# A ragged layer norm: who issues the first loads and the lengths, and TensorE's program unrolled in place of a loop

## The chip, the core and the metric

The kernel runs on one core of one Trainium2 chip. The metric is device time in microseconds (us). Before the change the median of three runs is 258.67 us (258.59 to 258.95).

## What is computed

`x` is a batch of 32 sequences of 512 rows with 1024 floats each; `lengths` says how many rows of each sequence are real (64 to 511).

```python
def reference(x, lengths, gamma, beta, eps):
    output = np.zeros_like(x)
    for b in range(batch):
        x_b = x[b, :lengths[b]]
        mean = np.mean(x_b, axis=-1, keepdims=True)
        var = np.var(x_b, axis=-1, keepdims=True)
        output[b, :lengths[b]] = (x_b - mean) / np.sqrt(var + eps) * gamma + beta
    return output
```

Rows past a sequence's length are zero, and need not be read.

## The kernel before

**Tiles.** A unit is 4 rows (16 KB). The first 64 rows of every sequence are always real; they make 4 static tiles of 128 units, one unit in each of the 128 partitions (2 MB a tile). All further units that hold a real row are numbered one after the other over the batch, from the lengths, and make the dynamic tiles; the units that hold none are filled from a tile of zeros `zt`, 128 units to a store. With the lengths of this run there are 19 tiles to normalize and 14 zero stores.

**Half tiles.** A tile is worked on as two half tiles (2 of its 4 rows in each partition; step `t`, 38 of them run). For each: VectorE (DVE) takes the row statistics (`dve_stats`, L396 and L401), ScalarE (ACT) takes the root (L423), DVE makes the reciprocal and the negated mean (L386, L387), ACT normalizes into fp16 `h` (L407), DVE multiplies by gamma (L380), TensorE (PE) adds beta by multiplying `h` with the identity and a row of ones with beta into PSUM (four matmuls each), and ACT writes PSUM back over `x` in SBUF, times the row mask (L416). Three `h` buffers, two PSUM buffers and eight `x` buffers rotate.

**What the lengths start.** DVE's first instruction that needs the lengths is the cast at L233, behind a few small ones that don't. Behind it stand, in DVE's program order, the sums over the lengths and the index tables (L234 to L269, the last one `idx_i`), the cast of the identity (L367), and only then the statistics of half tile 0, of half tile 1, the index of the first store and the masks (L334 to L329), and so on. GpSimd (POOL) waits for `idx_i` before it issues the loads of the dynamic tiles.

**Who issues what.** SyncE (SP) issues the two halves of tile 0 one after the other (L576): each is 1 MB, 8 KB in each partition, and has its own semaphore. ACT issues the lengths (L564: all 32 of them, as 256 bytes, into each of the 128 partitions), then gamma and beta (L565, L566: one partition, 4 KB each), and then starts its own program. POOL issues everything else as indirect DMAs: the loads of tiles 1 to 3 (static indices; L601), of tiles 4 to 7 once `idx_i` is there, then per tile a store (L623 for the two halves of tile 0, L630 for the others), at most one zero store (L637), and the load of the tile that reuses a freed buffer. Tile 1's store waits for the last write-back of half tile 3.

**TensorE's program.** For the 4 static tiles (6 half tiles) the instructions are written out (L442, L448), and wait for fixed counts of the semaphores. From there `run_tensor` runs a loop over three tiles (six half tiles, the period of the three `h` and two PSUM buffers): each half tile waits for counts kept in two registers, issues its eight matmuls (`emit_mm`, L433), adds 9 to the one and 5 to the other register, and after each tile branches on the number of tiles. The other engines have all tiles written out, with a conditional branch after each (`run_engine`).

Of the kernel before, what the change touches and what calls it, by code (L numbers as in the profile page):

```python
# [11 lines left out]
P = 128  # L12
UR = 4
ST_ROWS = 64
R = 8
RH = 3
RM = 4
DVE_STEP = 9
ACT_STEP = 5
ZSTEPS = (0, 1, 2, 3, 4, 5, 7, 9, 11, 13) + tuple(range(15, 32))  # L20

class Program:
# [46 lines left out]
def kernel(tc, x, lengths, gamma, beta, eps, out):  # L69
    nc = tc.nc  # L70
    B, T, D = x.shape
# [3 lines left out]
    NST = B * S0 // P  # L75
# [4 lines left out]
    NH = 2 * (NT + 1)  # L80
    CH = 512
    assert (B, T, D) == (32, 512, 1024)

    sem = {e: tc.alloc_semaphore(f"s_{e}") for e in ("DVE", "ACT", "PE", "POOL")}
    s_len = tc.alloc_semaphore("s_len")
    s_row = tc.alloc_semaphore("s_row")
    s_xs = [tc.alloc_semaphore(f"s_xs{i}") for i in range(2)]
# [13 lines left out]
    with pool_cm as sb, psum_cm as psb:  # L101
        def st(shape, dt, name):
            return sb.tile(shape, dt, name=name)

        xt = [st([P, UR * D], FP32, f"x{i}") for i in range(R)]
        ht = [st([P, 2, D], FP16, f"h{i}") for i in range(RH)]
        zt = st([P, UR * D], mybir.dt.bfloat16, "zt")
        len64 = st([P, B], mybir.dt.int64, "len64")
        row_f = st([1, 2 * D], FP32, "row_f")
        row_h = st([1, 2 * D], FP16, "row_h")  # L110
        gamma_h = st([P, D], FP16, "gamma_h")
        ones_h = st([1, P], FP16, "ones_h")
        idn_f = st([P, P], FP32, "idn_f")
        idn_h = st([P, P], FP16, "idn_h")
# [56 lines left out]
        ps = [psb.tile([P, 2, D], FP32, name=f"ps{i}") for i in range(2)]  # L171
# [4 lines left out]
        dve, act, pe, pool, sp = nc.vector, nc.scalar, nc.tensor, nc.gpsimd, nc.sync  # L176
        pr = Program(sem)
        add = pr.add

        def iota(t, pattern, base=0, mult=0):  # L180
# [9 lines left out]
            out=sidx[:, :], in0=p4_i[:, 0:1].broadcast_to([P, NST]), scalar=float(U - S0), in1=sb_i[:, :],  # L190
# [9 lines left out]
            out=idn_f[:, :], in_=idn_f[:, :], compare_op=OP.not_equal, fill=1.0,  # L200
            base=0, pattern=[[-1, P]], channel_multiplier=1), [a_i0])
        for t in range(2, R):
# [7 lines left out]
               for i, f in enumerate(fields)]  # L210
        d_k2 = add("DVE", lambda: dve.tensor_tensor(out=k_i[:, 0:2], in0=k_i[:, 0:2], in1=k_i[:, 2:4],
                                                    op=OP.bitwise_or), [d_k[3]])
        d_k1 = add("DVE", lambda: dve.tensor_tensor(out=k_i[:, 0:1], in0=k_i[:, 0:1], in1=k_i[:, 1:2],
                                                    op=OP.bitwise_or), [d_k2])
        d_dk = add("DVE", lambda: dve.tensor_tensor(out=dk_f[:, :], in0=k_i[:, 0:1], in1=p_i[:, :],
                                                    op=OP.subtract), [d_k1])
# [148 lines left out]
        tok = {}  # L365
# [58 lines left out]
                out=sq[r][:, :], in_=mv[r][:, :, 1], func=AF.Sqrt, bias=eps_sb[:, 0:1], scale=1.0),  # L424
                [tok["stats", t]])

        def emit_mm(t):
            h, p_ = ht[t % RH], ps[t % 2]
            for w, lhs in ((idn_h, None), (ones_h, row_h)):
                for j in range(2):  # L430
                    for c in range(2):
                        rhs = h[:, j, c * CH : c * CH + CH] if lhs is None else row_h[:, D + c * CH : D + c * CH + CH]
                        ins = pe.matmul(p_[:, j, c * CH : c * CH + CH], w[:, :], rhs,  # L433
                                        start=lhs is None, stop=lhs is not None)
            ins.then_inc(sem["PE"], 1)

        def pe_mm(t):
            h, p_ = ht[t % RH], ps[t % 2]
            first = [tok["mul", t], tok.get(("evac", t - 2)), tok["idn"], c_gam]
            for j in range(2):  # L440
                for c in range(2):
                    add("PE", lambda j=j, c=c: pe.matmul(  # L442
                        p_[:, j, c * CH : c * CH + CH], idn_h[:, :], h[:, j, c * CH : c * CH + CH],
                        start=True, stop=False), first, inc=False)
                    first = []
            for j in range(2):
                for c in range(2):
                    tok["pe", t] = add("PE", lambda j=j, c=c: pe.matmul(  # L448
                        p_[:, j, c * CH : c * CH + CH], ones_h[:, :], row_h[:, D + c * CH : D + c * CH + CH],
                        start=False, stop=True), [], inc=(j == 1 and c == 1))  # L450
# [22 lines left out]
        def emit_op(e, name, op):  # L473
            _, fn, waits, inc = op
            for key, val in waits:
                e.wait_ge(handles[key], val)
            ins = fn()
            if inc:
                ins.then_inc(sem[name], 1)

        def units_register(e, name):

            r = e.alloc_register(f"{name}_nd")
            e.wait_ge(sem["DVE"], d_tot[1])
            e.reg_load(r, tot_i[0:1, 0:1])
            return r

        def tiles_register(e, r):

            e.reg_add(r, r, P - 1)  # L490
            e.reg_alu(r, r, 7, OP.arith_shift_right)
            e.reg_add(r, r, NST)

        def run_engine(e, name, block, setup=None):
            base = nc.cur_bb
            guards = []
            r = None
            if setup is not None:
                setup()
            for op in pr.ops[name]:  # L500
                if op[0] == "op":
                    emit_op(e, name, op)
                else:
                    k = op[1]
                    if k == 2 * NST - 1:
                        r = units_register(e, name)
                        tiles_register(e, r)
                    if k >= 2 * NST + 1 and k % 2 == 1 and k < NH - 1:
                        nxt = f"{name}_s{k + 1}"
                        e.br_lt(r, (k + 1) // 2, f"{name}_exit", nxt)  # L510
                        for g in guards:
                            g.__exit__(None, None, None)
                        guards = [nc.bb(nxt, parent=base)]
                        guards[0].__enter__()
            e.br(f"{name}_exit")
            for g in guards:
                g.__exit__(None, None, None)
            with nc.bb(f"{name}_exit", parent=base):
                e.br(block.end_bb)

        def run_tensor(e, block):


            base = nc.cur_bb
            k0 = 2 * NST
            for op in pr.ops["PE"]:
                if op[0] == "op":
                    emit_op(e, "PE", op)
                elif op[1] == k0 - 1:
                    break  # L530
            r = units_register(e, "PE")
            tiles_register(e, r)
            r_dve, r_act, r_t = (e.alloc_register(f"PE_{n}") for n in ("dve", "act", "t"))
            e.reg_mov(r_dve, tok["mul", k0 - 2][1])
            e.reg_mov(r_act, tok["evac", k0 - 4][1])
            e.reg_mov(r_t, NST)
            for k in range(k0, NH):
                assert tok["mul", k - 2][1] == tok["mul", k0 - 2][1] + (k - k0) * DVE_STEP
                assert tok["evac", k - 4][1] == tok["evac", k0 - 4][1] + (k - k0) * ACT_STEP
            e.br("PE_s0")  # L540
            for i in range(3):
                with nc.bb(f"PE_s{i}", parent=base):
                    for k in (k0 + 2 * i, k0 + 2 * i + 1):
                        e.wait_ge(sem["DVE"], r_dve)
                        e.wait_ge(sem["ACT"], r_act)
                        emit_mm(k - 2)
                        e.reg_add(r_dve, r_dve, DVE_STEP)
                        e.reg_add(r_act, r_act, ACT_STEP)
                    e.reg_add(r_t, r_t, 1)
                    e.br_lt(r, r_t, "PE_exit", f"PE_s{(i + 1) % 3}")  # L550
            with nc.bb("PE_exit", parent=base):
                e.br(block.end_bb)

        with tc.tile_critical():
            with nc.Block() as block:

                @block.vector
                def _(e):
                    run_engine(e, "DVE", block)

                @block.scalar
                def _(e):
                    def setup():
                        e.dma_start(out=len64[:, :], in_=lengths[None, :].to_broadcast([P, B])).then_inc(s_len, 16)  # L564
                        e.dma_start(out=row_f[:, 0:D], in_=gamma[None]).then_inc(s_row, 16)  # L565
                        e.dma_start(out=row_f[:, D : 2 * D], in_=beta[None]).then_inc(s_row, 16)  # L566
                    run_engine(e, "ACT", block, setup)

                @block.tensor
                def _(e):  # L570
                    run_tensor(e, block)

                @block.sync
                def _(e):
                    for h in range(2):
                        e.dma_start(out=xt[0][:, 2 * h * D : 2 * h * D + 2 * D],  # L576
                                    in_=x[4 * h : 4 * h + 4, 0:ST_ROWS].rearrange("b (p r) d -> p b (r d)", r=2)
                                    ).then_inc(s_xs[h], 16)
                    e.br(block.end_bb)

                @block.gpsimd
# [139 lines left out]
```

## Time and profile before

| | |
|---|---|
| median of three runs | 258.67 us |
| the profiled execution's own time | 258.67 us |
| its span (first to last event on the core) | 256.5 us |
| busy in the span: PE, DVE, ACT, POOL | 55%, 70%, 71%, 25% |
| bytes moved by DMA | 105.37 MB, mean 411 GB/s |
| share of the span that DMA packets took: POOL's queue, SP's queue, ACT's queue | 95.9%, 2.1%, 0.1% |

A line of the timeline reads: start in us, duration, engine, line of the kernel, operation, out<-in, how many were merged (x2), and in brackets how long the engine had been idle and what ended that. ACTq, SPq and POOLq are the instruction queues of those engines, where DMAs are issued; the DMA queue of SP is numbered 1 in the page, that of ACT 10, that of POOL 0 and that of the instruction loads 14. In the list of DMA issues the last number is the time in us from issue to landing. In the table by stretches the last two columns are the DMA engines' busy share and GB/s. The trace also has every DMA packet with its queue, start, duration and size, and every step of a semaphore; where packets are spoken of, they are read there. Each of the 16 DMA engines serves all queues.

### The profile page before, as it was taken

The page shows a single profiled execution, that of the slowest core. Times are in us where ns is not written, and L with a number is a line of the kernel's source. Part 1 is how long each engine was busy: PE and PEld are TensorE (multiplying, and loading weights), DVE is VectorE, ACT ScalarE, POOL GpSimd, SP SyncE. Part 2 cuts the span into 40 slices and gives each one's busy share as a digit, 9 for nine tenths or more (in the row PEclk, how much of TensorE's full clock was granted, in tenths as well). Part 3 has the DMA queues.
Part 4 walks back from the last instruction along what each step waited for, and adds up shares of the span by engine and source line. Part 5 has one row for each costly group of instructions (what it writes and reads, how often), then busy time and mean ns, then how long its engine had stood idle before and what let it go on. Part 6 is the DMA issues. An engine that isn't in the chain of part 4 may idle for free.

```text
span 256.5 us, 1653 instructions
## 1 busy us (share of the span) xinstructions
PE 141.7 (55%) x306; PEld 32.4 (13%) x306; DVE 178.9 (70%) x421; ACT 182.9 (71%) x198; POOL 63.3 (25%) x68
## 2 busy tenths in 40 slices
PE   0101908274966678668767786687677867820000
PEld 0000202021211111111111111111111111100000
DVE  3989697987688778877887888678878886820000
ACT  2440756758799989998999899989998999850000
POOL 5183021040523322304112603040307130320000
DMA  4999999999999999999999999999999999999980
GB/s 167 435 437 423 432 424 418 438 434 432 423 443 416 443 419 439 422 437 437 422 429 424 437 424 423 429 436 424 439 419 437 422 437 419 445 423 434 427 353 10
DMA packets 8080, 105.37 MB, mean 411 GB/s; under 512 B 1388, under 2 KB 1388, under 8 KB 1390
## 3 DMA queue, kind: packets, MB, share of 16 engines
q0 software_dynamic: 7632, 103.13, 95.9%
q1 hardware_dynamic: 288, 2.10, 2.1%
q14 instruction: 11, 0.09, 0.1%
q10 hardware_dynamic: 148, 0.04, 0.1%
q8 instruction: 1, 0.02, 0.0%
HBM read 41.98 MB, written 69.21 MB: 433 GB/s over the span
## 4 chain that ended last, share of the span: by engine, by line
DVE 35%; PE 28%; ACT 18%; DMA 5%; issue 3%; POOLq 1%; ACTq 1%; SPq 0%; DVEq 0%; POOL 0%
PE ps_149 L433 23%; DVE stats_132 L396 18%; DMA x_61<-in_x_dram 5%; DVE h_69 L380 3%; DVE h_71 L380 3%; DVE h_70 L380 3%; ACT x_63 L416 3%; ACT x_62 L416 2%; ACT x_61 L416 2%; PE ps_149 L442 2%; PE ps_149 L448 2%; ACT x_68 L416 2%; ACT x_66 L416 2%; ACT x_67 L416 2%; ACT x_64 L416 2%
## 5 line engine op out<-in xcount | busy, mean ns | idle before, releaser
L433 PE MATMUL ps_150<-row_h,ones_h 1*128 1x512 f16 x64 | 30.1, 622 | 0.0
L433 PE MATMUL ps_149<-row_h,ones_h 1*128 1x512 f16 x64 | 30.1, 622 | 0.0
L433 PE MATMUL ps_149<-h_69,idn_h 128*128 128x512 f16 x24 | 11.3, 627 | 11.2 <-DVE h_69 L380 11.2
L380 DVE TENSOR_TENSOR h_69<-h_69,gamma_h 128x2048 f16<-128x2048 f16 x13 | 15.5, 1191 | 0.6 <-DVE mv_136 L401 0.6
L637 POOL DMA_INDIRECT out_dram<-zt,zidx x14 | 14.4, 1031 | 5.3 <-issue 4.0
L380 DVE TENSOR_TENSOR h_70<-h_70,gamma_h 128x2048 f16<-128x2048 f16 x13 | 15.5, 1189 | 0.0
L433 PE MATMUL ps_150<-h_70,idn_h 128*128 128x512 f16 x24 | 11.3, 626 | 6.8 <-DVE h_70 L380 6.8
L380 DVE TENSOR_TENSOR h_71<-h_71,gamma_h 128x2048 f16<-128x2048 f16 x12 | 14.3, 1190 | 0.0
L433 PE MATMUL ps_149<-h_71,idn_h 128*128 128x512 f16 x20 | 9.4, 627 | 8.6 <-DVE h_71 L380 8.6
L433 PE MATMUL ps_149<-h_70,idn_h 128*128 128x512 f16 x20 | 9.4, 627 | 7.9 <-DVE h_70 L380 7.9
L433 PE MATMUL ps_150<-h_71,idn_h 128*128 128x512 f16 x20 | 9.4, 628 | 6.3 <-DVE h_71 L380 6.3
L433 PE MATMUL ps_150<-h_69,idn_h 128*128 128x512 f16 x20 | 9.4, 628 | 6.3 <-DVE h_69 L380 6.3
L386 DVE RECIPROCAL rstd_143<-sq_139 128x2 f32<-128x2 f32 x10 | 1.7, 166 | 13.7 <-ACT sq_139 L423 13.7
L386 DVE RECIPROCAL rstd_141<-sq_137 128x2 f32<-128x2 f32 x10 | 1.7, 166 | 12.7 <-ACT sq_137 L423 12.7
L442 PE MATMUL ps_149<-h_69,idn_h 128*128 128x512 f16 x4 | 1.9, 628 | 14.5 <-DVE h_69 L380 14.5
L433 PEld LDWEIGHTS ps_150<-row_h,ones_h 1*128 1x128 f16 x64 | 6.7, 125 | 22.4 <-issue 22.4
L433 PEld LDWEIGHTS ps_149<-row_h,ones_h 1*128 1x128 f16 x64 | 6.7, 125 | 22.4 <-issue 22.4
L396 DVE BATCH_NORM_STATS2 stats_132<-x_61 128x6 f32<-128x512 f32 x12 | 7.4, 679 | 0.6 <-DMA x_61<-in_x_dram 0.6
L396 DVE BATCH_NORM_STATS2 stats_131<-x_62 128x6 f32<-128x512 f32 x12 | 7.4, 680 | 0.0
L396 DVE BATCH_NORM_STATS2 stats_131<-x_61 128x6 f32<-128x512 f32 x12 | 7.4, 680 | 0.0
L396 DVE BATCH_NORM_STATS2 stats_131<-x_63 128x6 f32<-128x512 f32 x12 | 7.4, 680 | 0.0
L396 DVE BATCH_NORM_STATS2 stats_131<-x_64 128x6 f32<-128x512 f32 x12 | 7.4, 680 | 0.0
(207 smaller groups left out, 384.2 us busy)
## 6 DMA issues: line engine op xcount, KB each, us to landing
x_61<-in_x_dram SPq DMA_DIRECT2D x2, 1024.0 KB, 10.6
out_dram<-zt,zidx POOLq DMA_INDIRECT x14, 23.7
len_73<-in_lengths_dram ACTq DMA_DIRECT2D x1, 32.0 KB, 4.4
x_65<-in_x_dram,idx_i POOLq DMA_INDIRECT x2, 20.3
x_66<-in_x_dram,idx_i POOLq DMA_INDIRECT x2, 19.7
x_67<-in_x_dram,idx_i POOLq DMA_INDIRECT x2, 21.7
x_68<-in_x_dram,idx_i POOLq DMA_INDIRECT x2, 23.7
out_dram<-x_61,fidx POOLq DMA_INDIRECT x2, 14.6
```

The source lines that it names most:

```text
L380: tok["mul", t] = add("DVE", lambda: dve.tensor_tensor(out=h[:, :, :], in0=h[:, :, :], in1=gamma_h[:, None, :].broadcast_to([P, 2, D]), op ...
L386: a = add("DVE", lambda: dve.reciprocal(out=rstd[r][:, :], in_=sq[r][:, :]), [tok["sqrt", t]])
L396: tk = add("DVE", lambda j=j, c=c: dve.bn_stats(out=s[:, j, c, :], in_=xx[:, j * D + c * CH : j * D + c * CH + CH]), [load_dep(t)])
L416: tok["evac", t] = add("ACT", lambda j=j, row=row: act.activation(out=xx[:, j * D : j * D + D], in_=p_[:, j, :], func=AF.Copy, bias=0.0, s ...
L433: ins = pe.matmul(p_[:, j, c * CH : c * CH + CH], w[:, :], rhs, start=lhs is None, stop=lhs is not None)
L442: add("PE", lambda j=j, c=c: pe.matmul(p_[:, j, c * CH : c * CH + CH], idn_h[:, :], h[:, j, c * CH : c * CH + CH], start=True, stop=False) ...
L448: tok["pe", t] = add("PE", lambda j=j, c=c: pe.matmul(p_[:, j, c * CH : c * CH + CH], ones_h[:, :], row_h[:, D + c * CH : D + c * CH + CH] ...
L637: e.indirect_dma_start(out=ou, out_offset=bass.IndirectOffsetOnAxis(ap=zidx[:, g : g + 1], axis=0), in_=zt[:, :], in_offset=None, bounds_c ...
```

## The change

TensorE's loop and what it needs go: PE runs through `run_engine` like the others, with all half tiles written out and fixed wait counts. The second half of tile 0 is issued by ACT ahead of gamma and beta; the lengths are issued by SP behind the first half.

```diff
+        def first_half(e, h):
+            e.dma_start(out=xt[0][:, 2 * h * D : 2 * h * D + 2 * D],
+                        in_=x[4 * h : 4 * h + 4, 0:ST_ROWS].rearrange("b (p r) d -> p b (r d)", r=2)
+                        ).then_inc(s_xs[h], 16)
...
-        def emit_mm(t):
...
-        def run_tensor(e, block):
...
                 @block.scalar
                 def _(e):
                     def setup():
-                        e.dma_start(out=len64[:, :], in_=lengths[None, :].to_broadcast([P, B])).then_inc(s_len, 16)
+                        first_half(e, 1)
                         e.dma_start(out=row_f[:, 0:D], in_=gamma[None]).then_inc(s_row, 16)
                         e.dma_start(out=row_f[:, D : 2 * D], in_=beta[None]).then_inc(s_row, 16)
                     run_engine(e, "ACT", block, setup)
 
                 @block.tensor
                 def _(e):
-                    run_tensor(e, block)
+                    run_engine(e, "PE", block)
 
                 @block.sync
                 def _(e):
-                    for h in range(2):
-                        e.dma_start(out=xt[0][:, 2 * h * D : 2 * h * D + 2 * D],
-                                    in_=x[4 * h : 4 * h + 4, 0:ST_ROWS].rearrange("b (p r) d -> p b (r d)", r=2)
-                                    ).then_inc(s_xs[h], 16)
+                    first_half(e, 0)
+                    e.dma_start(out=len64[:, :], in_=lengths[None, :].to_broadcast([P, B])).then_inc(s_len, 16)
                     e.br(block.end_bb)
```

The instructions of DVE and POOL and their order stay as they are, and so do ACT's behind its three issues; PE executes the same matmuls.

More of the change, by code (lines that the diff above doesn't have):

```diff
@@ L17 @@
 RM = 4
-DVE_STEP = 9
-ACT_STEP = 5
 ZSTEPS = (0, 1, 2, 3, 4, 5, 7, 9, 11, 13) + tuple(range(15, 32))
@@ L425, in act_sqrt @@
                 [tok["stats", t]])
-        def emit_mm(t):
[L428 to L435, printed above, removed]
         def pe_mm(t):
@@ L519, in run_engine @@
                 e.br(block.end_bb)
-        def run_tensor(e, block):
[L524 to L552, printed above, removed]
         with tc.tile_critical():
```

## Prediction

> **What bounds the kernel now.** I read the slices first, then the chain of waits, then the start of the timeline, then POOL's issues. The slices say that the DMA engines are busy from end to end, and the page's sums agree (POOL's queue alone 95.9% of the span).
>
> ```profile
> DMA  4999999999999999999999999999999999999980
> ...
> q0 software_dynamic: 7632, 103.13, 95.9%
> ```
>
> The bytes are fixed, so the time is the bytes' time plus whatever the DMA engines stand idle. They idle at the start (first slice 4 tenths) and in the last 4 us. In between, the question is where the stream is close to running dry. POOL issues all of it in time, except for one place. In the timeline of POOL and the list of DMA issues:
>
> ```profile
> 38.78 1.14 POOL L637 DMA_INDIRECT out_dram<-zt,zidx  x1 [1.32 <-DVE zidx L362]
> 50.76 0.99 POOL L630 DMA_INDIRECT out_dram<-x_62,sidx  x1 [10.84 <-ACT sq_138 L423]
> ```
> ```profile
> out_dram<-zt,zidx POOLq DMA_INDIRECT x14, 23.7
> out_dram<-x_62,sidx POOLq DMA_INDIRECT x1, 8.9
> ```
>
> Tile 1's store lands 8.9 us after its issue at 50.76; no other 2 MB transfer lands as soon. By the packets, its first one starts at 52.77, 2.01 us after the issue, just as the zero store ahead of it ends (53.31 on the last engine). 0.99 us of the 2.01 is the issue instruction itself. So between 0 and 1.02 us of backlog stood ahead of this store: were it later by more than that, the DMA engines would idle, and nothing later gives that back. Tile 2's store starts 3.25 us after its issue, tile 3's 6.92, later ones 11 to 29: behind this place there is cover, and the end is set by bytes.
>
> What leads up to 50.76 is compute without a pause. The chain of waits goes back to the load of tile 0:
>
> ```profile
> 1.61 13.97 DMA x_61<-in_x_dram
> 15.60 2.47 DVE stats_132 L396 x4
> ...
> 18.69 2.86 DVE f_f L296
> ```
>
> From 15.60 on it is only DVE, PE and ACT. So the start of the kernel is on the path, through tile 1's store, although DMA is the bound. And the start reads:
>
> ```profile
> 0.91 0.39 ACTq L564 DMA_DIRECT2D len_73<-in_lengths_dram  x1
> 0.95 1.24 SPq L576 DMA_DIRECT2D x_61<-in_x_dram  x2
> ...
> 5.30 0.18 DVE L233 CAST lenf<-len_73 128x32 f32<-128x32 int32 x1 [2.64 <-DMA len_73<-in_lengths_dram]
> ...
> 11.57 2.47 DVE L396 BATCH_NORM_STATS2 stats_131<-x_61 128x6 f32<-128x512 f32 x4
> ...
> 13.12 0.99 POOL L601 DMA_INDIRECT x_65<-in_x_dram,idx_i  x1 [5.30 <-DVE stats_131 L396]
> ...
> 15.60 2.47 DVE L396 BATCH_NORM_STATS2 stats_132<-x_61 128x6 f32<-128x512 f32 x4 [0.60 <-DMA x_61<-in_x_dram]
> ```
>
> DVE waits for the lengths until 5.30 (landed 5.28), works 6.3 us on indices without a gap, and only then starts half tile 0; POOL's loads of dynamic tiles hang on the same tables. Half tile 1 waits a further 0.6 us for its data.
>
> **The change part by part.**
>
> *The lengths, moved from the head of ACT's queue to behind 1 MB in SP's.* This is the term that counts. When do they land? By the packets, each of the 16 DMA engines carries 8 of the 128 length packets, 8 packets of 8 KB of each half of tile 0 (0.309 us each), and a closing 4-byte packet per transfer. In SP's queue the lengths come behind half 0 on every engine, and half 1 now competes from ACT's queue.
> - An engine's packets ran back to back from about 3.4 us (earliest) to 4.95 (latest) before, the late ones being those on which the lengths came late. I take the slowest engine at 3.6 to 4.9. By the time POOL's first packets come (7.23 to 8.04 before), an engine at 3.6 has done about 13 of its 16 packets of the two halves, one at 4.9 about 10.
> - From there queues alternate packet by packet: before, POOL's packets on one engine started every 0.913 us, that is one of 16 KB (0.611) and one of SP's 8 KB. So the last packets of half 0 and its closing one cost one turn of POOL each: half 0 closes at about 9.7 for the one engine, 11.7 for the other.
> - Then the eight lengths and their closing packet. **Two readings.** (a) In one turn: before, on all 16 engines, the first packet of x started 6 ns after the lengths' closing packet and none stood between; they ran as an unbroken nine. One turn of POOL (0.61) and 0.1 to 0.4 us for the nine (0.015 each, or the 0.055 at which the first engine's came), and 0.35 from last packet to semaphore (before: beta's 6.95 to 7.29): 10.8 to 13.1, middle 11.8. (b) Packet by packet: beta's closing packet came 0.30 us after its data had ended, one packet of x between; POOL's would cost nine turns of 0.625, 5.6 us: 15.7 to 17.7, middle 16.7.
> I take (a), as its row is of the lengths themselves, but x may not have been ready in time there, so (b) stays.
>
> The Trainium skill ("DMA: Bandwidth & Descriptors", section "Queues, rings and completion order") says that a DMA engine drains a whole packet of typically 9 to 17 descriptors from one queue before it switches. The alternation every 0.913 us is one descriptor each, so the trace does not show this for 8 KB and more; for the lengths the rule would give reading (a), and its sum.
>
> Everything in DVE's order behind the cast is later by what the lengths are later: 11.8 - 5.3 = 6.5 us (b: 11.4). Two things come off. Half tile 1's wait of 0.6 us for data vanishes, as half 1 lands with half 0; but the cast at 18.69 that takes 2.86 us ends with POOL's fill of `zt` (17.99 to 21.51), which moves with the indices, so the 0.6 may be lost there again: 0 to 0.6. And the backlog ahead of tile 1's store: 0 to 1.02. I take 0.8 for both. Tile 1's store, and from there the DMA stream to the end, is later by **5.7 us** (a: 5.5 - 1.6 = 3.9 to 7.8), or 10.6 (b: 10.4 - 1.6 = 8.8 to 12.4). On the way the loads of tiles 4 to 7 (13.12 before) would be issued at 19.6 (a) or 24.5 (b). Tile 3's load ended at 24.04, so (a) mostly escapes a gap there and (b) shows one of 2 to 3 us, which is part of its 10.6 and not on top.
>
> *Half 1 from ACT.* SP's second issue started 0.6 us behind the first; that is what two issuers save, and the lengths no longer stand in front of x (first x packets started 2.38 to 4.95, the lengths' first at 1.93). SP's queue had moved 0.70 MB by 6.0; at the later 430 GB/s from 3.4 on it would have been 1.12 MB, so x can stream up to 1 us sooner. This gives nothing: the gain only makes the stream wait longer at tile 1's store, which compute sets. The skill (same page, "Issuing engines are not separate DMA queues") speaks against the idea too: several issuers save issue time only. Its rule would leave the sum as it is.
>
> *Gamma and beta behind half 1.* They landed at 5.28 and 7.29; behind half 1 on one engine, with four turns of POOL, about 11 to 13.5. The copy (1.91), PE and the second copy (1.02) took 4.05 us from 7.31, so gamma is ready by 17.6; ACT's next work is the root at 14.31, now 20.8. Covered by 3 us; without that cover each us would count.
>
> *PE unrolled.* Cost 0. The eight matmuls take 3.7 us either way (1.89 + 1.83 written out, 3.71 in the loop), and start 0.04 us after the multiply in both (24.77 to 24.81; 63.58 to 63.62): the register waits cost nothing now, so their going gives nothing. 26 more half tiles of code at 16 instructions, at 90 KB for the 1653 of the page, are 23 KB, three 8 KB instruction packets of 0.31 us on one of 16 engines: 0.06 us. If PE waited for one (the longest took 0.94 us), tiles from 62 us on have 1 us of cover at tile 2's store, 5 at tile 3's and more later.
>
> **Sum.** The profiled execution took 258.67 us, equal to the median shown. 258.67 + 5.7 = **264.4**.
>
> **Rivals.**
> 1. *Lengths packet by packet (b)*: 258.67 + 10.6 = 269.3 (267.5 to 271.1). For it: the 0.913 us alternation, beta. Against: the unbroken nine. 0.33.
> 2. *Lengths sooner than (a)*, because POOL's first packets come later than 7.23 or the engines start evenly: half 0 landed at 8.2 with the engines nearly to itself, so 8.2 is a floor, 8.2 - 5.3 = 2.9, less 0.8, is 2.1 more: 260.8 (260.0 to 262.6). 0.11.
> 3. *Hidden*: DMA has 8 to 20 us of backlog in most of the run; if tile 1's store had it as well, 258.7. Against: 2.01 us. 0.03.
> 4. *Faster*: the lengths pass x on the engines, since an engine could take their small packets first, and land by about 6.3 (5.28 + 1.02); then x streams earlier and half tile 1 loses its wait. Up to the 1 us above: 257.7. It decides the sign at a landing of 6.3 to 6.9. Against: x closed no sooner than 6.0 on any engine, and the lengths stand behind it. 0.03.
>
> **Numbers.** (a) has 0.50, 262.6 to 266.5. Slower: 0.50 + 0.33 + 0.11 = 0.94; same 0.03; faster 0.03, where same means within 0.2% (0.5 us, about what can be told here). The range leaves out rivals 2 to 4 and little else: 262.3 to 270.8.
>
> **What would show it.** The cast of the lengths at 11 to 13 us (b: 16 to 18) in place of 5.30; half tile 0's statistics 6.3 us behind it; half tile 1 without a wait for data; gamma's copy before the first root; tile 1's store at 56 to 58 (b: 61 to 63), its first packet about 2 us behind, and slices below 9 around 53 to 58 us in the DMA row; PE's 3.7 us unchanged. Wrong if the store at L630 first starts more than 2.5 us after its issue, or lengths land before 9.

## The result, and the profile after

The changed kernel takes 269.08 us (median of 6 executions, 266.27 to 269.87); the kernel before takes 258.64 (6 executions beside it, 258.32 to 258.95). The ratio is 1.0376, 95% interval 1.0318 to 1.0434: the change costs 10.4 us by the medians, 9.7 by the ratio. Two of the six executions took 266.3, four about 269; the one profiled took 268.99 (span 267.0), so where the 266.3 came from was not seen.

The time is inside the stated range, but not where the forecast had put it: it is the first rival (269.3), not the likeliest case (264.4). The start of the changed kernel's timeline says why (the last line is the issue of tile 1's store; VectorE's idle time before the cast of the lengths stands in brackets):

```profile
0.92 0.66 ACTq L470 DMA_DIRECT2D x_61<-in_x_dram  x1
0.95 0.63 SPq L470 DMA_DIRECT2D x_61<-in_x_dram  x1
...
1.64 0.83 SPq L536 DMA_DIRECT2D len_73<-in_lengths_dram  x1
...
16.70 0.18 DVE L231 CAST lenf<-len_73 128x32 f32<-128x32 int32 x1 [14.04 <-DMA len_73<-in_lengths_dram]
...
22.95 2.47 DVE L394 BATCH_NORM_STATS2 stats_131<-x_61 128x6 f32<-128x512 f32 x4
...
24.50 0.99 POOL L559 DMA_INDIRECT x_65<-in_x_dram,idx_i  x1 [16.68 <-DVE stats_131 L394]
...
26.30 2.46 DVE L394 BATCH_NORM_STATS2 stats_132<-x_61 128x6 f32<-128x512 f32 x4
...
29.36 3.53 POOL L202 MEMSET zt<- 128x4096 bf16 x1
29.37 3.55 DVE L294 CAST f_f<-f_i 128x2 f32<-128x2 int32 x1
...
62.14 0.99 POOL L588 DMA_INDIRECT out_dram<-x_62,sidx  x1 [10.84 <-ACT sq_138 L421]
```

The lengths are awaited until 16.70 in place of 5.30. The indices follow without a gap, half tile 0 begins 6.25 us behind the cast as before, and half tile 1 (26.30) no longer waits for its data. In the list of DMA issues (last number: us to landing) the halves and the lengths read:

```profile
x_61<-in_x_dram ACTq DMA_DIRECT2D x1, 1024.0 KB, 5.4
x_61<-in_x_dram SPq DMA_DIRECT2D x1, 1024.0 KB, 9.2
...
len_73<-in_lengths_dram SPq DMA_DIRECT2D x1, 32.0 KB, 15.0
...
out_dram<-x_62,sidx POOLq DMA_INDIRECT x1, 7.1
```

Two transfers of 1 MB issued 0.03 us apart land 4 us apart: they did not move side by side. Tile 1's store lands 7.1 us after its issue, where it took 8.9 before: nothing stood ahead of it any more. The slices of the page show the stretches in which the stream had run dry, and in the table by stretches (the last two columns are the DMA engines' busy share and GB/s) they can be dated:

```profile
DMA  6997999954999999999999999999999999999990
```
```profile
23.00:24.00 1.00, 0.00 (x0) 0.00 (x0) 1.00 (x3) 0.00 (x0) 0.00 (x0) 1.00 0.84 360
24.00:25.00 1.00, 0.00 (x0) 0.00 (x0) 1.00 (x3) 0.00 (x0) 0.50 (x1) 1.00 0.08 33
25.00:26.00 1.00, 0.00 (x0) 0.00 (x0) 0.66 (x3) 0.30 (x1) 0.70 (x2) 1.00 0.00 0
...
56.00:58.00 2.00, 2.00 (x5) 0.42 (x4) 1.39 (x4) 1.57 (x3) 0.00 (x0) 1.00 0.40 156
58.00:60.00 2.00, 0.18 (x1) 0.00 (x0) 1.92 (x9) 2.00 (x3) 0.00 (x0) 1.00 0.00 0
60.00:62.00 2.00, 0.00 (x0) 0.00 (x0) 2.00 (x3) 1.53 (x3) 0.00 (x0) 1.00 0.00 0
62.00:64.00 2.00, 0.00 (x0) 0.00 (x0) 1.93 (x5) 0.00 (x0) 1.56 (x2) 1.00 0.31 131
```

In the mean over the 16 engines, some 2 us are idle ahead of tile 4's load, whose issue waited for the indices, and some 6.5 between 56 and 64 ahead of tile 1's store, while compute worked on. By the packets, no engine moves anything from 24.73 to 26.18 and from 58.15 to 63.70. From there to the end the stream is full in both kernels. Step by step, in us from each span's start (landings and first packets from the trace's semaphore steps and packets):

| event | before | after | later by |
|---|---|---|---|
| last length packet landed | 5.28 | 16.68 | 11.40 |
| half tile 0's statistics begin | 11.57 | 22.95 | 11.38 |
| half tile 1's statistics begin | 15.60 | 26.30 | 10.70 |
| the cast f_f ends (with POOL's fill of zt) | 21.54 | 32.92 | 11.38 |
| tile 1's store is issued | 50.76 | 62.14 | 11.38 |
| its first packet on each of the 16 engines starts: first, last (mean) | 52.44, 54.22 (53.11) | 63.70, 63.85 (63.76) | 10.65 |
| last packet of POOL's queue ends | 252.36 | 262.80 | 10.44 |
| the profiled execution | 258.67 | 268.99 | 10.32 |

Before the change the engines come to tile 1's store at different times: each goes on to it when the zero store ahead has ended there, which its 4-byte closing packet marks, and the 16 closing packets start from 52.44 to 54.22. The 52.77 of the prediction is another thing: it is the start of the packet that would be the store's first if POOL's packets were counted over all engines in order of start. Where all engines stand idle the two agree, as at 63.70 in the changed kernel.

### The profile page after: what moved, and what is told of

It is laid out like the page before. It is cut to its first block, busy times and chain, and to the rows that moved or that the text cites. A ratio compares the mean times of both kernels' runs of the same rounds, so it can differ in the third digit from the quotient of the medians.

```text
span 267.0 us, 1586 instructions
## 1 busy us (share of the span) xinstructions
PE 141.7 (53%) x306; PEld 32.4 (12%) x306; DVE 179.5 (67%) x421; ACT 182.9 (68%) x198; POOL 64.6 (24%) x68
## 4 chain that ended last, share of the span: by engine, by line
DVE 37%; PE 26%; ACT 17%; DMA 6%; issue 3%; POOLq 0%; ACTq 0%; SPq 0%; DVEq 0%; POOL 0%
DVE stats_132 L394 17%; PE ps_149 L430 13%; PE ps_149 L436 13%; DMA len_73<-in_lengths_dram 6%; DVE h_69 L378 3%; DVE h_71 L378 3%; DVE h_70 L378 3%; ACT x_63 L414 2%; ACT x_62 L414 2%; ACT x_61 L414 2%; ACT x_66 L414 2%; ACT x_68 L414 2%; ACT x_67 L414 2%; ACT x_64 L414 2%; ACT x_65 L414 2%
## 5 line engine op out<-in xcount | busy, mean ns | idle before, releaser
L436 PE MATMUL ps_150<-row_h,ones_h 1*128 1x512 f16 x76 | 35.8, 622 | 0.0
L436 PE MATMUL ps_149<-row_h,ones_h 1*128 1x512 f16 x76 | 35.8, 622 | 0.0
L430 PE MATMUL ps_149<-h_69,idn_h 128*128 128x512 f16 x28 | 13.2, 627 | 36.8 <-DVE h_69 L378 36.8
L430 PE MATMUL ps_149<-h_71,idn_h 128*128 128x512 f16 x24 | 11.3, 627 | 15.3 <-DVE h_71 L378 15.3
L430 PE MATMUL ps_149<-h_70,idn_h 128*128 128x512 f16 x24 | 11.3, 627 | 13.8 <-DVE h_70 L378 13.8
L430 PE MATMUL ps_150<-h_70,idn_h 128*128 128x512 f16 x28 | 13.2, 627 | 7.0 <-DVE h_70 L378 7.0
L595 POOL DMA_INDIRECT out_dram<-zt,zidx x14 | 15.2, 1088 | 5.3 <-issue 4.0
L430 PE MATMUL ps_150<-h_71,idn_h 128*128 128x512 f16 x24 | 11.3, 627 | 6.6 <-DVE h_71 L378 6.6
L430 PE MATMUL ps_150<-h_69,idn_h 128*128 128x512 f16 x24 | 11.3, 626 | 6.5 <-DVE h_69 L378 6.5
L421 ACT ACTIVATE sq_137<-mv_133,eps_sb 128x2 f32<-128x2 f32 x10 | 2.9, 293 | 14.0 <-DVE mv_133 L399 14.0
L436 PEld LDWEIGHTS ps_149<-row_h,ones_h 1*128 1x128 f16 x76 | 7.9, 125 | 26.6 <-issue 26.6
L436 PEld LDWEIGHTS ps_150<-row_h,ones_h 1*128 1x128 f16 x76 | 7.9, 125 | 26.6 <-issue 26.6
L430 PEld LDWEIGHTS ps_149<-h_69,idn_h 128*128 128x128 f16 x28 | 3.0, 130 | 47.0 <-DVE h_69 L378 43.1
L559 POOL DMA_INDIRECT x_65<-in_x_dram,idx_i x2 | 2.6, 1284 | 22.5 <-DVE stats_131 L394 16.7
L394 DVE BATCH_NORM_STATS2 stats_132<-x_63 128x6 f32<-128x512 f32 x12 | 7.4, 680 | 0.0
L394 DVE BATCH_NORM_STATS2 stats_131<-x_62 128x6 f32<-128x512 f32 x12 | 7.4, 680 | 0.0
```

What stands on the lines that cost most here:

```text
L394: tk = add("DVE", lambda j=j, c=c: dve.bn_stats(out=s[:, j, c, :], in_=xx[:, j * D + c * CH : j * D + c * CH + CH]), [load_dep(t)])
L421: tok["sqrt", t] = add("ACT", lambda: act.activation(out=sq[r][:, :], in_=mv[r][:, :, 1], func=AF.Sqrt, bias=eps_sb[:, 0:1], scale=1.0), [ ...
L430: add("PE", lambda j=j, c=c: pe.matmul(p_[:, j, c * CH : c * CH + CH], idn_h[:, :], h[:, j, c * CH : c * CH + CH], start=True, stop=False) ...
L436: tok["pe", t] = add("PE", lambda j=j, c=c: pe.matmul(p_[:, j, c * CH : c * CH + CH], ones_h[:, :], row_h[:, D + c * CH : D + c * CH + CH] ...
L559: e.indirect_dma_start(out=xt[t % R][:, :], out_offset=None, in_=xu, in_offset=bass.IndirectOffsetOnAxis(ap=column(t), axis=0), bounds_che ...
L595: e.indirect_dma_start(out=ou, out_offset=bass.IndirectOffsetOnAxis(ap=zidx[:, g : g + 1], axis=0), in_=zt[:, :], in_offset=None, bounds_c ...
```

## Experiments

Theory after the result: each of the nine length packets of an engine waits for one 16 KB packet of POOL, so the lengths are 11.4 us late; compute up to tile 1's store is late by as much; the stream has 0.45 us of cover there (2.01 - 1.56), and the rest goes to the end. (The 2.01 rests on the counted 52.77; by the engines the cover is about 0.1 to 1.9 us, see the next section. The expectations of runs 5 and 6 still use 0.45.) Rivals: the written-out TensorE program has a share; standing behind 1 MB costs by itself, whatever POOL does; two issuers of the halves are themselves slow; the loss is in the order of the DMA queues and not in the late start of compute. Where nothing else is said, TensorE is written out and the rest is as in the kernel before. Ratios are to the kernel before on the same chip, whose median was 259.40 us for the first four runs, 258.80 for the next four and 259.24 for the last four.

**1. TensorE written out, alone** (e1)
```diff
-                    run_tensor(e, block)
+                    run_engine(e, "PE", block)
```


> TensorE written out, loads and lengths issued as before. Theory (the lengths' landing is all of it): 258.7 us, within 0.3, the eight matmuls of a half tile still 3.7 us. Rival (the longer program costs instruction loads or waits): 0.5 us or more above 258.7, with PE idle at instruction loads.

Measured: 259.22 us, ratio 0.9994 (0.9983 to 1.0006). PE is busy 141.7 us as in both other kernels. The trace has three more instruction packets of 16 KB (queue 8, 0.9 to 1.0 us each) than that of before, as it has in the changed kernel; they cost nothing that can be measured.

**2. Loads and lengths moved, TensorE's loop kept** (e2): the diff of the change without its TensorE part.

> TensorE's loop kept, loads and lengths issued as in the changed kernel. Theory: the changed kernel's time, 266 to 270 us, lengths landing at about 16.7. Rival (the longer TensorE program has a share of the loss): clearly below 266.

Measured: 269.96 us, ratio 1.0403 (1.0381 to 1.0424). The lengths land at 17.39. Runs 1 and 2 together put the whole loss on the moved transfers.

**3. The lengths between the halves, all three on SyncE** (e3)
```diff
-                        e.dma_start(out=len64[:, :], in_=lengths[None, :].to_broadcast([P, B])).then_inc(s_len, 16)
...
-                    for h in range(2):
...
+                    first_half(e, 0)
+                    e.dma_start(out=len64[:, :], in_=lengths[None, :].to_broadcast([P, B])).then_inc(s_len, 16)
+                    first_half(e, 1)
```


> SyncE issues half 0, the lengths and half 1 in this order; ScalarE only gamma and beta; TensorE written out. The lengths still stand behind 1 MB of half 0, but half 1 doesn't come before them, so they should reach the engines before POOL's first packets at about 7.0. Theory (each length packet pays a turn of POOL's 16 KB): lengths land at 6 to 7, about 1 to 1.7 later than before, time 259.2 to 260.2. Rival (standing behind 1 MB is by itself what costs): lengths at 9 or later, time 262 or more.

Measured: 260.87 us, ratio 1.0055 (1.0037 to 1.0074). The lengths land at 8.06, later than I expected and sooner than the rival did, and the time is between the two as well. The length packets start from 5.31 to 7.76: 2.5 us for 128 small packets with POOL's first packet only at 8.63. So 2.8 us of the delay is the place behind 1 MB and the lengths' own time; the 8.6 us from there to 16.68 is something else.

**4. The lengths at ScalarE's head, the halves from two issuers** (e4)
```diff
                         e.dma_start(out=len64[:, :], in_=lengths[None, :].to_broadcast([P, B])).then_inc(s_len, 16)
+                        first_half(e, 1)
...
-                    for h in range(2):
...
+                    first_half(e, 0)
```


> ScalarE issues the lengths, half 1, gamma, beta; SyncE half 0; TensorE written out: both halves are issued at once, as in the change, but the lengths stay at the head. Theory: lengths land at 5.3, time 258.7 within 0.5. Rival (two issuers of the halves are themselves slow or fast): a time more than 0.5 away from 258.7 with the lengths still at 5.3.

Measured: 259.55 us, ratio 1.0003 (0.9992 to 1.0014), lengths at 5.51. The two issuers neither gain nor lose. In its list of issues the halves, issued 0.40 us apart, land 7.5 (half 0) and 14.6 us (half 1) after their issues. By the packets, half 1's first starts at 5.99, when 98 of half 0's 128 have started.

**5 and 6. Nothing moved, VectorE delayed by one and by four repeats of a comparison** (e5 as shown, e6 with range(4))
```diff
+            for _ in range(1):
+                d_cmp = add("DVE", lambda: dve.tensor_tensor(
+                    out=c3, in0=q_f[:, lo:hi, None].broadcast_to([P, n, B]),
+                    in1=cum[:, None, :].broadcast_to([P, n, B]), op=OP.is_ge), [d_cmp])
```


> Issue order as before, TensorE written out, one comparison of the index tables (1.13 us of DVE) done twice. Theory (the stream has 0.45 us of cover at tile 1's store, and every further delay of DVE's start goes to the end): plus 1.1 - 0.45 = 0.7 us, 259.4. Rival (the loss of the changed kernel came from the order of the DMA queues, not from the late start of compute): 258.7.

> The same with four repeats, 4.5 to 4.7 us more of DVE ahead of half tile 0. Theory: half tile 1's wait for data (0.6 us) vanishes but is given back at the fill of zt, so plus 4.6 - 0.45 = 4.1 us, 262.8, the DMA row below 9 just ahead of tile 1's store. Rival: 258.7 to 260.

Measured: 259.56 us, ratio 1.0028 (1.0016 to 1.0041), 0.76 us more; and 262.72, ratio 1.0153 (1.0128 to 1.0178), 3.92 more. The timeline of the longer one shows the added work and the store that it delays, its slices the hole:

```profile
8.86 4.60 DVE L264 TENSOR_TENSOR cmp<-q_f,cum 128x928 f32<-128x928 f32 x4
...
55.44 0.99 POOL L634 DMA_INDIRECT out_dram<-x,sidx  x1 [10.83 <-ACT sq L427]
```
```profile
DMA  4999999949999999999999999999999999999990
```

4.60 us of work at 8.86 make tile 1's store 4.68 late (50.76 to 55.44), and the end is late by 3.9. In run 5 1.16 us of work make the store 1.64 late (52.40), and the end is late by 0.76. So 0.8 and 0.9 us are lost on the way, more than the 0.45 of the theory. In both runs the first packet that starts behind the pause does so 1.56 us after the issue. No queue order was touched, so the late start of compute is by itself enough to make the end late.

**7. POOL's fill of zt moved into its wait for the indices** (e7)
```diff
         for t in range(2, R):
+            if t == NST:
+                a_zt = add("POOL", lambda: pool.memset(zt[:, :], 0.0))
             pr.raw("POOL", ("load", t))
-        a_zt = add("POOL", lambda: pool.memset(zt[:, :], 0.0))
```


> Issue order as before, TensorE written out; POOL fills zt while it waits for the indices (7.8 to 11.3) in place of behind the loads. Theory: the 2.9 us that DVE stood at the cast f_f goes, tile 1's store is issued at about 48 and first moves at 52.8 as before, so the time stays at 258.7 within 0.3 (bytes bound it). Rival (compute up to tile 1's store sets the end by itself): 2 to 2.9 us faster. It may go wrong if the fill slows the index tables in turn.

Measured: 258.95 us, ratio 1.0006 (0.9995 to 1.0018). It settles nothing between the two, since tile 1's store did not come sooner (51.46):

```profile
7.82 3.54 POOL L204 MEMSET zt<- 128x4096 bf16 x1
...
11.72 1.12 DVE L261 TENSOR_TENSOR cmp<-q_f,cum 128x928 f32<-128x928 f32 x1
...
22.07 0.17 DVE L297 CAST f_f<-f_i 128x2 f32<-128x2 int32 x1
```

The cast f_f takes 0.17 us in place of 2.85, but the index tables now stand still during the fill: the comparison starts at 11.72, not 7.64. VectorE paid for the fill in both places.

**8. The same move in the changed kernel** (e9), where VectorE is idle from 7.8 to 11.4.

> The changed kernel with POOL's fill of zt moved ahead of the loads of tiles 4 to 7. Theory: DVE's 3.55 us at the cast f_f goes, tile 1's store moves from 62.1 to 58.6, and the time falls by the same 3.5 us from 269.1 to 265.6. Rival (the loss is in the DMA order or at the loads of tiles 4 to 7): 268 or more.

Measured: 266.47 us, ratio 1.0288 (1.0266 to 1.0310), 2.6 us below the changed kernel. Its timeline shows the cast and the store:

```profile
29.96 0.17 DVE L295 CAST f_f<-f_i 128x2 f32<-128x2 int32 x1
...
59.35 0.99 POOL L589 DMA_INDIRECT out_dram<-x,sidx  x1 [10.83 <-ACT sq L422]
```

The lengths landed 0.6 us later than in the profile of the changed kernel (17.27), the cast f_f took 0.17, and tile 1's store was issued 2.8 us sooner. The median alone would not show the gain, since two executions of the changed kernel took 266.3 as well. In the profiled executions POOL's last packet ends at 260.48 in place of 262.80: the end went with the store, though no load of a dynamic tile and no length came sooner.

**9. Half 1 issued by ScalarE behind gamma and beta** (e10)
```diff
-                        first_half(e, 1)
                         e.dma_start(out=row_f[:, 0:D], in_=gamma[None]).then_inc(s_row, 16)
                         e.dma_start(out=row_f[:, D : 2 * D], in_=beta[None]).then_inc(s_row, 16)
+                        first_half(e, 1)
```
(shown against the changed kernel)

> As the changed kernel, but ScalarE issues half 1 behind gamma and beta, at about 1.9 us, so behind the lengths' issue on SyncE. Theory (transfers of SyncE and ScalarE move in the order of their issue, one after the other, as half 1 and half 0 did in the changed kernel): half 0, lengths, half 1 as in the run with the lengths between the halves: lengths land at about 8, time 260.2 to 261. Rival (the two queues move side by side): the lengths take turns with half 1 and then with POOL, landing at 10 or later, 262.5 or more.

Measured: 260.64 us, ratio 1.0051 (1.0033 to 1.0069). The lengths land at 8.15, half 1's first packet starts at 7.28. The order of issue decides: the same two engines issue the same transfers as in the changed kernel, and of its 10.4 us all but 1.4 are gone with half 1 issued 0.8 us later (1.72 in place of 0.92). POOL's first packet, too, comes later, at 8.91 in place of 7.03 (8.63 in run 3), though issued at the same time, so the lengths are through before any of POOL's; why it comes later the traces do not show.

**10. The changed kernel, POOL waiting for the lengths before its first load** (e11)
```diff
                         if t == 1:
                             wait(a_sidx)
+                            wait(("len", 16))
```


> The changed kernel, with POOL waiting for the lengths before it issues its first load. Theory (each length packet waits for one 16 KB packet of POOL): without POOL's packets the lengths land at 8.5 to 9.5, DVE starts 3.2 to 4.2 later than before, and the time is 262 to 263 although POOL's loads start 6 us later. Rival (the late landing is from standing behind 1 MB in the queue): lengths at 12 or later, 265 or more.

Measured: 263.87 us, ratio 1.0171 (1.0152 to 1.0191).

```profile
8.89 0.18 DVE L231 CAST lenf<-len 128x32 f32<-128x32 int32 x1 [6.23 <-DMA len<-in_lengths_dram]
9.87 1.20 POOL L559 DMA_INDIRECT x<-in_x_dram,sidx  x1 [8.52 <-DVE un L236]
```

The lengths stand where they stand in the changed kernel, behind half 0, which stands behind half 1; without POOL's packets they land at 8.87, 7.8 us sooner, 1.5 of them because half 0 does not meet POOL's packets either (it lands at 8.70, not 10.18). All 128 move between 7.81 and 8.46. The time is 0.9 above what I expected: POOL's first packet comes at 11.78, so the stream idles for 3.3 us and is then itself the later one (at tile 1's store, issued at 55.14, the engines are still busy with the zero store ahead until 57.25 to 59.16).

**11. The changed kernel with the lengths as one packet** (e13): they are loaded into one partition, cast to fp16 (all are at most 511), spread by a matmul with a row of ones, and copied from PSUM.
```diff
-e.dma_start(out=len64[:, :], in_=lengths[None, :].to_broadcast([P, B])).then_inc(s_len, 16)
+e.dma_start(out=len64[0:1, :], in_=lengths[None, :]).then_inc(s_len, 16)
...
+        d_lh = add("DVE", lambda: dve.tensor_copy(out=len_h[:, :], in_=len64.bitcast(INT32)[:, 0::2]), [("len", 16)])
+        e_len = add("PE", lambda: pe.matmul(ps[1][:, 0, 0:B], ones_h[:, :], len_h[:, :], start=True, stop=True),
+                    [d_lh, d_one])
...
-        d_len = add("DVE", lambda: dve.tensor_copy(out=lenf[:, :], in_=len64.bitcast(INT32)[:, 0::2]), [("len", 16)])
+        d_len = add("DVE", lambda: dve.tensor_copy(out=lenf[:, :], in_=ps[1][:, 0, 0:B]), [e_len])
```


> The changed kernel with the lengths as one packet in the same place behind half 0, spread by TensorE. Theory (a packet behind POOL's pays one turn of 0.63 us, so two turns in place of nine): lengths land at 9.5 to 11, the cast follows 0.6 later, the time is 263 to 264.7. Rival (the place behind half 0 costs, not the number of packets): above 267.

Measured: 265.71 us, ratio 1.0242 (1.0224 to 1.0259). The packet starts at 11.28 and lands at 12.26, later than I expected, because half 0 closed later on its engine (landing 11.45); the copy comes 0.49 behind, and the time is 1.0 above the expected range. Counted from half 0's landing, the one packet takes 0.81 us, the 128 took 6.50 in the changed kernel (6.44 and 6.11 in runs 2 and 8). Its engine has two turns (the data and the closing packet) where it had nine, so seven turns cost 5.3 to 5.7 us, 0.76 to 0.81 each: a little more than one POOL packet, which took 0.61 to 0.95 us there in the changed kernel (0.68 in the mean).

**12. The kernel before with the lengths as one packet at ScalarE's head** (e12): the edit of run 11 alone.

> Issue order as before, TensorE written out, but the lengths are loaded into one partition (one packet of 256 bytes), cast to fp16, spread over the partitions by one matmul with a row of ones, and copied from PSUM. Theory: the lengths land at about 2.8 and are spread by 3.5, 1.8 sooner than before; the packets of half 0 no longer wait behind 128 small ones and the stream is 0.5 to 1 us ahead; tile 1's store comes early enough to keep it so: 257.7 to 258.2 where before is 258.7, that is 0.2 to 0.4% faster. Rival (the start of the stream doesn't reach the end): the same time within 0.2%.

Measured: 258.82 us, ratio 0.9981 (0.9963 to 0.9999): 0.4 us faster than before, at the edge of what can be told: 0.2% is the least that was expected and the most that the rival allows.

```profile
2.60 0.13 DVE L225 CAST len_h<-len 1x32 f16<-1x32 int32 x1
...
3.02 0.19 DVE L237 COPY lenf<-ps 128x32 f32<-128x32 f32 x1 [0.30 <-PE ps L226]
...
49.26 0.99 POOL L634 DMA_INDIRECT out_dram<-x,sidx  x1 [10.83 <-ACT sq L427]
```

The lengths are spread by 3.2, tile 1's store is issued 1.5 us sooner, and by 7.0 us 1.67 MB have moved where it was 1.19. That lead is 1.1 us of stream. With POOL's data packets counted over all engines in order of start, it is 0.5 at the 385th, where tile 4 begins (22.94, before 23.43), and none at the 897th, where the first store begins (43.00, before 43.02), though that store was issued at 30.03. Where the lead goes stays open. It is the one version here whose interval lies below the kernel before, if barely.

## Why the prediction was right about the sign and wrong about the case

- **What bounds the kernel** was right: a stream of fixed bytes with one thin place, tile 1's store, which compute sets. How thin it was the prediction read wrongly. The zero store ahead was not through at 53.31: the engines left it between 52.44 and 54.22, and it landed at 54.70. Where the stream had run dry, the store's packets start 1.56 to 1.71 us after its issue (1.62 in the mean). So the cover was not one number from 0 to 1.02 but some 0.1 us on the first engine and up to 1.9 on the last, 0.7 in the mean (53.11 - 50.76 - 1.62). The run times agree: the store's lateness less the loss is 0.9 in run 5, 0.8 in run 6 and 0.9 to 1.0 in runs 8 and 11 and the changed kernel (1.3 to 1.5 in runs 2, 3 and 9, which no run explains). The starts that the prediction gives for later stores are counted like the 52.77.
- **The step that failed** is the choice of reading (a), "in one turn": it put the landing at 11.8 and the time at 264.4, 4.7 us short. The lengths took turns packet by packet, reading (b). The row that (a) rested on, nine length packets unbroken on all 16 engines before x, did not show that small packets hold an engine against another queue. In runs 4 and 9 and the changed kernel, too, a transfer from SyncE or ScalarE sent its first packets only when most of those of the transfer issued ahead of it on the other queue were out (half 0's first at 4.67 behind half 1's from 2.35; half 1's at 5.99 in run 4, half 0's being three quarters out). So x may not have been there to take turns. That is argued, not shown: on every engine x's first packet follows the start of the lengths' closing packet by 6 ns, which fits an x that had to wait as well as one that came behind. I had named that doubt and weighed it too low; beta's closing packet was the row of a true turn. The Trainium skill's rule of 9 to 17 descriptors per turn ("DMA: Bandwidth & Descriptors", section "Queues, rings and completion order") does not fit these 256-byte packets: from 9.3 us on 16 KB packets of POOL's start right behind them (0.012 us in the median), and an engine's nine turns take 6.7 us in the mean.
- **That (b) was met so closely is luck.** Its 16.7 for the landing was measured as 16.68 and its 269.3 as 269.08, but two of its terms were off in opposite directions. Half 0 closed on the engines at 8.67 to 9.87, not at 9.7 to 11.7. The nine turns took 6.7 us in the mean, not 5.6; POOL's packets took 0.61 to 0.95 us in that stretch, not 0.61 throughout. With the same transfers runs 2 and 8 land at 17.39 and 17.27, and the executions of the changed kernel lie between 266.3 and 269.9.
- **"Half 1 now competes"** was wrong in the same way. The halves shared the engines only for the last 16 of half 1's 128 packets; half 1, issued 0.03 us ahead, went first (landing 6.30) and half 0, which is needed first, second (10.18, before 8.20). For the lengths it came to the same, as both halves were ahead of them.
- **Gamma and beta** were put at 11 to 13.5; the copy of them starts at 7.63, since half 1 had been first. Covered either way.
- **What comes off**: 0.8 us was taken, and it was about that, all of it cover. Half tile 1's wait of 0.6 vanished and was given back at the fill of zt, as the lower bound had it (the cast f_f took 3.55 in place of 2.85). The store was issued 11.38 late, its first packets start 10.65 late in the mean, and POOL's queue ends 10.44 later. The last 0.2 us is less than such ends differ from profile to profile (252.36 before, 252.67 in run 1).
- **The stream starts sooner** by 1.76 - 1.19 = 0.57 MB at 7.0 us, and it gives nothing, as said: it idles for longer at 24 to 26 and at 58 to 64.
- **PE at no cost** was right (run 1: 0.9994), though the instruction packets were three of 16 KB and 0.9 to 1.0 us each, not three of 8 KB and 0.31.

## What to carry to other kernels

A few bytes on which the order of everything else hangs belong at the head of a queue, in as few packets as can be. Behind two megabytes and beside a queue of 16 KB packets, 32 KB in 128 packets took 15 us to land; as one packet of 256 bytes, spread by a matmul, the same lengths took 10.6; 128 packets at the head took 4.4. A kernel whose DMA queues are busy for 98% of the span can still be set by compute: look for the transfer that lands soonest after its issue, since there the stream is about to run dry, and price a delay by what still stands in front of that one, on each engine. Two transfers issued at once from two engines need not move at once; see in the packets which one is first before counting on the order.

## What the runs showed of the hardware that was not expected

- A 1 MB transfer from SyncE or ScalarE moved behind the one issued just ahead of it on the other of the two queues, even 0.03 us later: its first packet came when 112 of the 128 packets ahead had started (changed kernel, runs 2, 8, 9, 10 and 11) or 98 (run 4). With the lengths ahead of half 0 in the kernel before it was so on each engine alone: half 0's first packet came at 2.38, when 39 of the 128 length packets had started, but on no engine before the lengths were through there.
- 128 packets of 256 bytes, with no packet of POOL's among them, start over 2.5 to 3.2 us (1.93 to 4.92 before; 1.95 to 5.15 in run 4; 5.31 to 7.76 in run 3), but over 0.65 where both halves were ahead of them (7.81 to 8.46 in run 10). The engines can thus take them at the faster pace; that their preparation sets the slower one fits this, but the traces do not show it.
- An indirect DMA whose queue has run dry moves its first packet 1.56 us after its issue starts, 0.99 of it the instruction (tile 1's store in the eight kernels in which the stream had run dry there, 1.56 to 1.57), but the first one of all takes 4.3 to 6.3 us where POOL issues it at 2.6, and 1.92 where it is issued at 9.87 (run 10).
- POOL's fill of zt (3.53 us) stops VectorE at some instructions until it ends (the cast f_f: 0.17 us without it, 1.9 to 3.55 with it; the index tables in run 7), while a few small ones pass.
